# A 16-wide substitution whose blocks are joined on TensorE, as a stage of its own in the next iteration of a gated-delta-rule mixer

## Chip, cores and metric

One core of a Trainium2 chip runs the whole model, six feed-forward and mixer layers and a second model of two mixers, in one launch. The metric is the device time of one execution in microseconds. The engines are PE (TensorE; PEld is its weight load), DVE (VectorE), ACT (ScalarE), POOL (GpSimd), and SP, which issues the DMAs.

## What is computed

The change lies in one layer, the gated delta rule: 512 positions, 16 value heads of width 128 over 8 query and key heads. Cut to what matters (the kernel works in chunks of 128 positions):

```python
decay = exp(where(lower, g[..., :, None] - g[..., None, :], -inf))
kb, vb = k * beta[..., None], v * beta[..., None]
L = where(strict, einsum('bhncd,bhnsd->bhncs', kb, k) * decay, 0.0)
T = triangular_solve(eye + L, eye, lower=True, unit_diagonal=True)
u, w = T @ vb, T @ (kb * exp(g)[..., None])
...
def step(state, inp):
    v_new = u_n - w_n @ state
    o = q_n @ state + a_n @ v_new
    state = state * gl_n + k_n.T @ v_new
```

The inverse of the unit triangular matrix `eye + L`, one 128x128 block for each head and chunk, is what the edited code computes.

## The kernel before

All activations are held with the channel on the partitions, and a weight matmul is done as three in a reduced-precision format: high by high, low by high, high by low (`mm3`, L145 to L147). A weight tile comes in by SP (`raw`, three buffers), ACT rounds it to `wh` (L139) and DVE forms the rest `wl` (L140). Results land in `acc`, three banks of PSUM; DVE or ACT must read a bank before PE may fill it again.

`gdn` works in 8 groups `gi`, of one query and key head and two value heads. `stage_a` projects and convolves the group's queries and keys, normalises them (`norms`), forms their products with themselves (L1099, masked on DVE to `gt` at L1100), and from them the strictly triangular blocks `Am` (L1120, L1121, four operations on DVE) and `At` (POOL, L1122), 8 blocks of 128x128 side by side. Then it inverts. Each 128x128 block has four 32x32 blocks on its diagonal. Through DRAM (`ad`) they are laid out so that each partition holds whole 32x32 blocks (`ai`), and a substitution runs along the rows of the unknowns `ui`, which start as parts of the identity. First the two 16-wide halves are done at once, 15 steps of a product and a sum (L1142, L1144); then the upper half is tied to the lower with two large products (L1148, L1149), and 15 more steps finish it (L1151, L1153). Back through DRAM (`ud`, `uc`), a transpose on DVE gives `tcp` (L1164), and PE joins 32-wide blocks to 64 (L1180, L1185, L1188) and 64 to 128 (L1194, L1197), with ACT copying the results from the bank `mg` between (to `z32`, `tz`, `U`).

`stage_v` projects and convolves the values (transposed at L1211); `stage_b` runs the recurrence over the four chunks: `k` times the state `St` (L1238), `R` on DVE (L1240), `U` times `R` (L1243), `vnew` on ACT (L1246), the state's increment and the output (L1250 to L1254), the new `St` on DVE (L1259; L1262 a copy for the first chunk). `stage_z` is the output gate, `stage_g` normalises the output, and `stage_o` is the output projection of the group before, added into `h` on DVE (L1292), 8 times a group.

The loop emits, in iteration `gi`: values of `gi+1`, `stage_a` of `gi+2`, recurrence of `gi`, gate, norm, projection of `gi-1`. Before it stand `stage_a` of 0 and 1 and the values of 0. This order is a priority alone: a scheduler that has its own notion of how long things take places each instruction in its engine's queue when the program is built, and each engine then works strictly through its queue. Pools decide too: `Am`, `U`, `ui` have two buffers, `big` (for `ai`, the broadcast gates and the norms) three, `mg` one bank.

Of the kernel before, what the change touches and what calls it, by code (L numbers as in the profile page):

```python
# [12 lines left out]
AF = mybir.ActivationFunctionType  # L13
ALU = mybir.AluOpType
AX = mybir.AxisListType
# [951 lines left out]
def gdn(self, feed0, gate, tail):  # L967
    nc, tc, A = self.nc, self.tc, self.A
    with tc.tile_pool(name="gd", bufs=1) as gd, tc.tile_pool(name="gdd", bufs=1, space=bass.MemoryType.DRAM) as dr:
# [104 lines left out]
        def stage_a(gi):  # L1074
# [19 lines left out]
            q, k = qk  # L1094
# [33 lines left out]

            ad = dr.tile([8, 4, 32, 32], F32, name="ad", bufs=2)
# [6 lines left out]
            nc.vector.memset(ai.rearrange("p j i -> p (j i)")[:, 0:1024:33], -1.0)  # L1136
            ui = T("ui", (P, 8, 32), bufs=2)
            nc.sync.dma_start(ui, A["gdn_eye"])
            mt = T("mt", (P, 2, 4, 16), bufs=2)
# [6 lines left out]
            for v in range(2):  # L1146
                x = T("ix").rearrange("p (q i j) -> p q i j", q=4, i=8)
                nc.vector.tensor_mul(x, fdims(ui, 0, (32, 4), (0, 8), (1, 16)), fdims(ai, 16 + 8 * v, (0, 4), (1, 8), (32, 16)))  # L1148
                nc.vector.tensor_reduce(ui[:, 0:4, 16 + 8 * v:24 + 8 * v], x, axis=AX.X, op=ALU.add, negate=True)  # L1149
            for t in range(1, 16):  # L1150
                nc.vector.tensor_mul(mt[:, 0, :, :t + 1], ui[:, 0:4, 16:17 + t],  # L1151
                                     fdims(ai, 16 * 32 + 16 + t, (0, 4), (32, t + 1)))
                nc.vector.tensor_reduce(ui[:, 0:4, 16 + t:17 + t], mt[:, 0, :, :t + 1], axis=AX.X, op=ALU.add, negate=True)  # L1153
# [9 lines left out]
            tcp = T("tcp", (P, 8, 32))  # L1163
            nc.vector.transpose(tcp.rearrange("p n i -> p (n i)"), uc.rearrange("p n i -> p (n i)"))  # L1164
# [4 lines left out]
            for b in range(4):  # L1169
                sl = slice(32 * b, 32 * b + 32)  # L1170
                nc.scalar.copy(U[sl, :, sl], uc[sl])
                if b < 2:
                    nc.scalar.copy(t64[sl, :, sl], tcp[sl])
            n8 = "p (n i) -> p n i"
            z32 = T("z32", (P, 8, 32))
            pm = self.bank("mg")
            for m in range(2):
                s0, s1 = slice(64 * m, 64 * m + 32), slice(64 * m + 32, 64 * m + 64)
                for n in range(8):
                    nc.tensor.matmul(pm[s1, n * 32:(n + 1) * 32], Am[s0, n, s1], tcp[s0, n, :], start=True, stop=True)  # L1180
                nc.scalar.copy(z32[s1], pm[s1, 0:256].rearrange(n8, n=8))
# [563 lines left out]
```

## Time and profile before

| | |
|---|---|
| median of 3 runs | 2827.94 us (2823.83 to 2828.90) |
| the profiled execution | 2832.52 us |
| its span | 2830.7 us, 36488 instructions |
| mean granted clock of PE | 0.971 |
| this layer | about 1850 to 2480 us of the span |

The span is what the profile shows, from the first instruction to the last; the execution's time has 1.8 us more. An engine's busy time is the time in which one of its instructions ran. A wait is put down to the instruction whose end released it. Granted clock 1.00 is 2.4 GHz and 0.50 is 1.2 GHz.

### The profile page before, as it was taken

The numbers are of one execution on the slowest core, as the hardware profiler recorded it, in microseconds if no ns is written. First come the engines' busy times: TensorE is split into PE (matmuls) and PEld (weight loads), VectorE is DVE, ScalarE is ACT, GpSimd is POOL, SyncE is SP. The second block draws the span as 40 slices with busy tenths as digits, with TensorE's granted clock in tenths as the row PEclk, the third lists the DMA queues.
The fourth block names the chain that finished last, engine by engine and source line by source line (L and its number), as shares of the span: only waits on it lengthen the run. The fifth ranks groups of instructions, "written<-read, shape, count | busy, mean of one in ns | idle before, by whom it ended". The sixth has DMA issues, their size and how long they took to land.

```text
span 2830.7 us, 36488 instructions
## 1 busy us (share of the span) xinstructions
PE 2718.2 (96%) x13879; PEld 2218.0 (78%) x13879; DVE 1774.8 (63%) x3321; ACT 1194.0 (42%) x2192; POOL 239.4 (8%) x224
## 2 busy tenths in 40 slices
PE   8999999999999999999899999988999999999998
PEld 6888878788888888887678888876777777777776
DVE  6454577754545644358854343599778788577765
ACT  4222254532323422233463232374545444477773
POOL 0000002000000000005310000030111111120001
PEclk9999999999999999999999999999889999899999
DMA  5343332244443433322113333323223233132221
GB/s 184 116 139 108 125 93 75 90 134 120 133 127 106 137 103 97 96 87 86 50 60 94 100 95 99 92 66 113 76 86 105 88 96 89 43 99 68 78 63 62
DMA packets 106704, 274.49 MB, mean 97 GB/s; under 512 B 35465, under 2 KB 39553, under 8 KB 106529
## 3 DMA queue, kind: packets, MB, share of 16 engines
q1 hardware_dynamic: 106528, 272.15, 31.3%
q8 instruction: 110, 1.80, 0.3%
q14 instruction: 66, 0.53, 0.1%
HBM read 267.79 MB, written 4.31 MB: 96 GB/s over the span
## 4 chain that ended last, share of the span: by engine, by line
PE 35%; DVE 10%; ACT 3%; issue 1%; POOL 1%; DMA 0%; DVEq 0%; SPq 0%; POOLq 0%; ACTq 0%
PE acc L145 9%; PE acc L146 9%; PE acc L147 9%; DVE wl L140 1%; PE mg L1484 1%; POOL x L1389 1%; DVE Am L1121 1%; DVE mt L1142 0%; PE sb L1475 0%; PE mg L1185 0%; DVE Am L1120 0%; ACT wh L139 0%; PE mg L1194 0%; PE sb L1254 0%; PE sb L1243 0%
## 5 line engine op out<-in xcount | busy, mean ns | idle before, releaser
L145 PE MATMUL acc<-xh,wh 128*128 128x512 f32 (+2 forms) x2320 | 914.5, 395 | 18.9 <-ACT xh L186 8.2
L146 PE MATMUL acc<-xl,wh 128*128 128x512 f32 (+1 forms) x2320 | 906.9, 391 | 5.4 <-POOL xl L151 3.2
L147 PE MATMUL acc<-xh,wl 128*128 128x512 f32 (+1 forms) x2320 | 903.3, 390 | 2.0 <-DVE wl L140 2.0
L139 ACT CAST wh<-raw 128x1024 fp32r<-128x1024 f32 (+3 forms) x430 | 439.3, 1022 | 1076.7 <-PE acc L146 713.3
L140 DVE TENSOR_TENSOR wl<-raw,wh 128x1024 fp32r<-128x1024 f32 (+2 forms) x410 | 488.1, 1192 | 97.0 <-ACT wh L139 93.2
L145 PEld LDWEIGHTS acc<-xh,wh 128*128 128x128 f32 (+1 forms) x2320 | 438.2, 189 | 110.5 <-ACT xh L186 8.2
L146 PEld LDWEIGHTS acc<-xl,wh 128*128 128x128 f32 x2320 | 438.2, 189 | 95.0 <-POOL xl L151 4.5
L147 PEld LDWEIGHTS acc<-xh,wl 128*128 128x128 f32 x2320 | 437.6, 189 | 92.4 <-DVE wl L140 3.5
L146 PE MATMUL acc<-al,wh 128*128 128x512 f32 (+1 forms) x720 | 278.1, 386 | 0.0
L147 PE MATMUL acc<-ah,wl 128*128 128x512 f32 (+1 forms) x720 | 277.8, 386 | 0.0
L145 PE MATMUL acc<-ah,wh 128*128 128x512 f32 (+1 forms) x720 | 277.4, 386 | 0.0
L249 DVE SCALAR_TENSOR_TENSOR h<-acc,h 128x512 f32<-128x512 f32 x128 | 88.4, 690 | 215.7 <-PE acc L147 215.3
L289 DVE TENSOR_TENSOR tmp<-acc,rstd 128x512 f32<-128x512 f32 x88 | 60.9, 691 | 240.0 <-PE acc L147 240.0
L287 DVE TENSOR_TENSOR tmp<-acc,rstd 128x512 f32<-128x512 f32 x88 | 60.8, 691 | 176.2 <-PE acc L147 176.1
L146 PEld LDWEIGHTS acc<-al,wh 128*128 128x128 f32 x720 | 135.2, 188 | 28.6 <-DVE al L151 0.8
L145 PEld LDWEIGHTS acc<-ah,wh 128*128 128x128 f32 x720 | 135.2, 188 | 28.2
L147 PEld LDWEIGHTS acc<-ah,wl 128*128 128x128 f32 x720 | 135.2, 188 | 28.0
L145 PE MATMUL acc<-ogh,wh 128*128 128x512 f32 (+1 forms) x256 | 111.5, 440 | 19.4 <-DVE h L1292 19.2
L140 POOL TENSOR_TENSOR wl<-raw,wh 128x1024 fp32r<-128x1024 f32 (+1 forms) x20 | 47.8, 2393 | 872.2 <-ACT wh L139 861.2
L146 PE MATMUL acc<-ogl,wh 128*128 128x512 f32 (+1 forms) x256 | 106.4, 416 | 0.0
L147 PE MATMUL acc<-ogh,wl 128*128 128x512 f32 (+1 forms) x256 | 105.0, 410 | 0.0
L150 ACT CAST ah<-tmp 128x512 fp32r<-128x512 f32 x88 | 54.8, 623 | 63.9 <-DVE tmp L290 63.9
(448 smaller groups left out, 3589.0 us busy)
## 6 DMA issues: line engine op xcount, KB each, us to landing
raw<-in_wi_dram SPq DMA_DIRECT2D x176, 512.0 KB
raw<-in_wo_dram SPq DMA_DIRECT2D x64, 512.0 KB
raw<-in_ada_w_dram SPq DMA_DIRECT2D x48, 512.0 KB
raw<-in_a_in_dram SPq DMA_DIRECT2D x48, 512.0 KB
raw<-in_b_in_dram SPq DMA_DIRECT2D x24, 512.0 KB
raw<-in_wo_dram SPq DMA_DIRECT2D x24, 384.0 KB
raw<-in_a_out_dram SPq DMA_DIRECT2D x16, 512.0 KB
big<-rd SPq DMA_DIRECT2D x13, 512.0 KB
```

Of the source, the lines that this page charges most:

```text
L139: nc.scalar.copy(wh[:, :n], raw[:, :n])
L140: self.lo_eng.tensor_tensor(wl[:, :n], raw[:, :n], f32(wh[:, :n]), op=ALU.subtract)
L145: nc.tensor.matmul(out, ah, bh, start=start, stop=False)
L146: nc.tensor.matmul(out, ah, bl, start=False, stop=False)
L147: nc.tensor.matmul(out, al, bh, start=False, stop=stop)
L150: self.nc.scalar.copy(hi, x)
L249: nc.vector.scalar_tensor_tensor(self.h[m], ps, scale(m), self.h[m], op0=ALU.mult, op1=ALU.add)
L287: nc.vector.tensor_mul(t, pg, rstd)
L289: nc.vector.tensor_mul(u, pu, rstd)
L1121: nc.vector.tensor_mul(m, m, bcol[:, :, hs[a]:hs[a] + 1].to_broadcast([P, 4, P]))
L1389: nc.gpsimd.tensor_mul(x, x, r)
L1484: nc.tensor.matmul(po[pair[a], j * P:], vs[p][:, j, vo:vo + 64], pT[a][:, j, j * P:], start=j == 0, stop=j == 3)
```

## The change

The substitution stops after the 15 steps of the two 16-wide halves. PE joins the halves: in each of the four 32-partition strips, `Am` of the lower rows times `tcp` (L1172, 32 matmuls), an ACT copy to `z32`, `z32` times the upper half of `uc` (L1176, 32 matmuls), a subtraction on DVE (L1178) and a second transpose. The old joining then follows, with the two strips of a batch now alternating, so that its five batches of 32-wide blocks become two. All of this, from the substitution on, is a function of its own, `stage_u`. In iteration `gi` it is emitted for group `gi+1` behind the recurrence of `gi`; for group 0 it stands between the two `stage_a` ahead of the loop.

```diff
--- before.py
+++ after.py
@@ -1126,6 +1126,7 @@
                 nc.gpsimd.tensor_mul(qd[:, a], q, gbc[:, a])
 
 
             ad = dr.tile([8, 4, 32, 32], F32, name="ad", bufs=2)
             for b in range(4):
                 nc.sync.dma_start(ad[:, b].rearrange("n j i -> j n i"), Am[32 * b:32 * b + 32, :, 32 * b:32 * b + 32])
@@ -1133,9 +1134,13 @@
             adv = ad.rearrange("n b j i -> (n b) (j i)")
             for s in range(4):
                 nc.sync.dma_start(ai[32 * s:32 * s + 32].rearrange("p j i -> p (j i)"), adv)
-            nc.vector.memset(ai.rearrange("p j i -> p (j i)")[:, 0:1024:33], -1.0)
             ui = T("ui", (P, 8, 32), bufs=2)
             nc.sync.dma_start(ui, A["gdn_eye"])
+            return dict(hs=hs, k=k, knat=knat, egl=egl, ekd=ekd, At=At, qd=qd, Am=Am, ai=ai, ui=ui)
+
+        def stage_u(d):
+            Am, ai, ui = d["Am"], d["ai"], d["ui"]
+            nc.vector.memset(ai.rearrange("p j i -> p (j i)")[:, 0:1024:33], -1.0)
             mt = T("mt", (P, 2, 4, 16), bufs=2)
             for t in range(1, 16):
                 nq = (t + 3) // 4
@@ -1143,14 +1148,6 @@
                                      fdims(ai, t, (528, 2), (0, nq), (32, t + 1)))
                 nc.vector.tensor_reduce(fdims(ui, t, (144, 2), (32, nq), (1, 1)), mt[:, :, :nq, :t + 1], axis=AX.X,
                                         op=ALU.add, negate=True)
-            for v in range(2):
-                x = T("ix").rearrange("p (q i j) -> p q i j", q=4, i=8)
-                nc.vector.tensor_mul(x, fdims(ui, 0, (32, 4), (0, 8), (1, 16)), fdims(ai, 16 + 8 * v, (0, 4), (1, 8), (32, 16)))
-                nc.vector.tensor_reduce(ui[:, 0:4, 16 + 8 * v:24 + 8 * v], x, axis=AX.X, op=ALU.add, negate=True)
-            for t in range(1, 16):
-                nc.vector.tensor_mul(mt[:, 0, :, :t + 1], ui[:, 0:4, 16:17 + t],
-                                     fdims(ai, 16 * 32 + 16 + t, (0, 4), (32, t + 1)))
-                nc.vector.tensor_reduce(ui[:, 0:4, 16 + t:17 + t], mt[:, 0, :, :t + 1], axis=AX.X, op=ALU.add, negate=True)
             ud = dr.tile([8, 4, 8, 4, 32], F32, name="ud", bufs=2)
             for s in range(4):
                 nc.sync.dma_start(ud[:, :, :, s].rearrange("n b q i -> (n b) q i"), ui[32 * s:32 * s + 32])
@@ -1160,34 +1157,50 @@
             uc = T("uc", (P, 8, 32))
             for b in range(4):
                 nc.sync.dma_start(uc[32 * b:32 * b + 32], udv[b])
-            tcp = T("tcp", (P, 8, 32))
-            nc.vector.transpose(tcp.rearrange("p n i -> p (n i)"), uc.rearrange("p n i -> p (n i)"))
+            n8 = "p (n i) -> p n i"
+            z32, tcp = T("z32", (P, 8, 32)), T("tcp", (P, 8, 32))
+
+            def turned():
+                nc.vector.transpose(tcp.rearrange("p n i -> p (n i)"), uc.rearrange("p n i -> p (n i)"))
+            quart = [slice(32 * b, 32 * b + 32) for b in range(4)]
+
+            turned()
+            pm = self.bank("mg")
+            for n in range(8):
+                for q in quart:
+                    r = slice(q.start, q.start + 16)
+                    nc.tensor.matmul(pm[q, n * 32:(n + 1) * 32], Am[r, n, q], tcp[r, n, :], start=True, stop=True)
+            nc.scalar.copy(z32, pm[:, 0:256].rearrange(n8, n=8))
+            for n in range(8):
+                for q in quart:
+                    nc.tensor.matmul(pm[q, 256 + n * 16:256 + (n + 1) * 16], z32[q, n, :], uc[q, n, 16:32], start=True,
+                                     stop=True)
+            nc.vector.tensor_sub(uc[:, :, 16:32], uc[:, :, 16:32], pm[:, 256:384].rearrange(n8, n=8))
+            turned()
             lo, hi = slice(0, 64), slice(64, P)
             tz = T("tz", (P, 8, 64))
             t64, z64 = tz[lo], tz[hi]
             nc.gpsimd.memset(t64, 0.0)
-            for b in range(4):
-                sl = slice(32 * b, 32 * b + 32)
-                nc.scalar.copy(U[sl, :, sl], uc[sl])
+            for b, q in enumerate(quart):
+                nc.scalar.copy(U[q, :, q], uc[q])
                 if b < 2:
-                    nc.scalar.copy(t64[sl, :, sl], tcp[sl])
-            n8 = "p (n i) -> p n i"
-            z32 = T("z32", (P, 8, 32))
+                    nc.scalar.copy(t64[q, :, q], tcp[q])
             pm = self.bank("mg")
-            for m in range(2):
-                s0, s1 = slice(64 * m, 64 * m + 32), slice(64 * m + 32, 64 * m + 64)
-                for n in range(8):
+            both = ((quart[0], quart[1]), (quart[2], quart[3]))
+            for n in range(8):
+                for s0, s1 in both:
                     nc.tensor.matmul(pm[s1, n * 32:(n + 1) * 32], Am[s0, n, s1], tcp[s0, n, :], start=True, stop=True)
+            for s0, s1 in both:
                 nc.scalar.copy(z32[s1], pm[s1, 0:256].rearrange(n8, n=8))
-            for m in range(2):
-                s0, s1 = slice(64 * m, 64 * m + 32), slice(64 * m + 32, 64 * m + 64)
-                for n in range(8):
+            for n in range(8):
+                for s0, s1 in both:
                     nc.tensor.matmul(pm[s0, n * 32:(n + 1) * 32], z32[s1, n, :], uc[s1, n, :], start=True, stop=True)
-                if m == 0:
-                    for n in range(8):
-                        nc.tensor.matmul(pm[s1, 256 + n * 32:256 + (n + 1) * 32], uc[s1, n, :], z32[s1, n, :],
-                                         start=True, stop=True)
-                    nc.scalar.activation(t64[s1, :, s0], pm[s1, 256:512].rearrange(n8, n=8), AF.Copy, scale=-1.0)
+            s0, s1 = both[0]
+            for n in range(8):
+                nc.tensor.matmul(pm[s1, 256 + n * 32:256 + (n + 1) * 32], uc[s1, n, :], z32[s1, n, :], start=True,
+                                 stop=True)
+            nc.scalar.activation(t64[s1, :, s0], pm[s1, 256:512].rearrange(n8, n=8), AF.Copy, scale=-1.0)
+            for s0, s1 in both:
                 nc.scalar.activation(U[s0, :, s1], pm[s0, 0:256].rearrange(n8, n=8), AF.Copy, scale=-1.0)
             pm = self.bank("mg")
             for n in range(8):
@@ -1196,7 +1209,7 @@
             for n in range(8):
                 nc.tensor.matmul(pm[lo, n * 64:(n + 1) * 64], z64[:, n, :], U[hi, n, hi], start=True, stop=True)
             nc.scalar.activation(U[lo, :, hi], pm[lo].rearrange(n8, n=8), AF.Copy, scale=-1.0)
-            return dict(hs=hs, k=k, knat=knat, egl=egl, ekd=ekd, At=At, qd=qd, U=U)
+            d["U"] = U
 
         def stage_v(gi):
             hs = (2 * gi, 2 * gi + 1)
@@ -1292,7 +1305,9 @@
                     nc.vector.scalar_tensor_tensor(self.h[m], ps, gate[:, m:m + 1], self.h[m], op0=ALU.mult, op1=ALU.add)
 
         og, last = {}, []
-        st = {gi: stage_a(gi) for gi in range(2)}
+        st = {0: stage_a(0)}
+        stage_u(st[0])
+        st[1] = stage_a(1)
         vs = {0: stage_v(0)}
         for gi in range(8):
             if gi < 7:
@@ -1302,6 +1317,8 @@
             if gi == 0:
                 self.late()
             oT = stage_b(gi, st.pop(gi), vs.pop(gi))
+            if gi < 7:
+                stage_u(st[gi + 1])
             z = stage_z(gi)
             og[gi] = stage_g(gi, oT, z)
             if gi:
```

Three places in the order that the scheduler makes of it. First DVE, where the products of one group (`gt`, `Am`) meet the additions into `h` of the projection. Before, group 6's products:

```order
L1292 SCALAR_TENSOR_TENSOR h_89<-acc,mod_273,h_89 128x512
L1100 TENSOR_TENSOR gt<-sa,dmask 128x512 x2
L1120 TENSOR_TENSOR Am<-gt,tmp 128x512 x2
L1121 TENSOR_TENSOR Am<-Am,gbcol 128x512 x2
L1044 TENSOR_TENSOR nr_17816<-nr_17815 128x8
L1292 SCALAR_TENSOR_TENSOR h_90<-acc,mod_273,h_90 128x512
L1045 TENSOR_TENSOR nr_17816<-nr_17816,nr_17814 128x8
L1292 SCALAR_TENSOR_TENSOR h_91<-acc,mod_273,h_91 128x512
```

Now, the corresponding place of group 6 (L1305 is the old L1292, L1288 the old L1275):

```order
L1100 TENSOR_TENSOR gt<-sa,dmask 128x512 x2
L1120 TENSOR_TENSOR Am<-gt,tmp 128x512
L140 TENSOR_TENSOR wl<-raw,wh 128x1024
L1121 TENSOR_TENSOR Am<-Am,gbcol 128x512
L1120 TENSOR_TENSOR Am<-gt,tmp 128x512
L1121 TENSOR_TENSOR Am<-Am,gbcol 128x512
L1288 TENSOR_TENSOR oT<-oT,zg 128x512
L1016 SCALAR_TENSOR_TENSOR zg<-zg,acc 128x512
L1288 TENSOR_TENSOR oT<-oT,zg 128x512
L1305 SCALAR_TENSOR_TENSOR h_89<-acc,mod_273,h_89 128x512
L1040 TENSOR_SCALAR nr_17850<-nr_17850 128x8
```

Before, the first `h` stands ahead of the four `Am` and the other seven behind; now all eight stand behind.

Second PE, at a joining in the later groups. Before (L1180 to L1188 are batches of eight small matmuls between the large ones of a projection):

```order
L1180 MATMUL mg<-tcp,Am 32x32 x8
L146 MATMUL acc<-xl_106,wh 128x512
L147 MATMUL acc<-xh_98,wl 128x512
L145 MATMUL acc<-xh_99,wh 128x512
L146 MATMUL acc<-xl_107,wh 128x512
L147 MATMUL acc<-xh_99,wl 128x512
L1180 MATMUL mg<-tcp,Am 32x32 x8
L145 MATMUL acc<-xh_100,wh 128x512
L146 MATMUL acc<-xl_108,wh 128x512
L147 MATMUL acc<-xh_100,wl 128x512
L1185 MATMUL mg<-uc,z_15440 32x32 x8
L1188 MATMUL mg<-z_15440,uc 32x32 x8
```

Now (L1251, L1256, L1263, L1266 and L1267 are the recurrence, the old L1238, L1243, L1250, L1253 and L1254):

```order
L1256 MATMUL sb<-R,U 128x128 x2
L1172 MATMUL mg<-tcp,Am 32x32 x25
L1263 MATMUL sb<-vnew,kdec 128x128 x2
L1266 MATMUL sb<-qd,St 128x128
L1267 MATMUL sb<-At,vnew 128x128
L1266 MATMUL sb<-qd,St 128x128
L1267 MATMUL sb<-At,vnew 128x128
L1172 MATMUL mg<-tcp,Am 32x32 x2
L1061 MATMUL sa<-ident,nr_17401 8x128
L1172 MATMUL mg<-tcp,Am 32x32 x5
L147 MATMUL acc<-xh_102,wl 128x512
L145 MATMUL acc<-xh_103,wh 128x512
```

The joining of one group has moved from beside a projection into the recurrence of the group before, and its first new batch is broken up by it. Over all groups PE goes over to 32- or 64-wide matmuls 45 times before and 77 times now.

Third DVE, around the first `St` of group 0's recurrence. Before:

```order
L1022 SCALAR_TENSOR_TENSOR x_15195<-acc,pk,x_15195 128x511
L1153 TENSOR_REDUCE ui<-mt 128x4
L1022 SCALAR_TENSOR_TENSOR x_15195<-acc,pk,x_15195 128x510
L1151 TENSOR_TENSOR mt<-ui,big 128x4x11
L1022 SCALAR_TENSOR_TENSOR x_15195<-acc,pk,x_15195 128x509
L1153 TENSOR_REDUCE ui<-mt 128x4
L1262 COPY St<-sb 128x128
L1151 TENSOR_TENSOR mt<-ui,big 128x4x12
L1262 COPY St<-sb 128x128
```

Now (L1275 is the old L1262, L1253 the old L1240):

```order
L1100 TENSOR_TENSOR gt<-sa,dmask 128x512
L1120 TENSOR_TENSOR Am<-gt,tmp 128x512
L1100 TENSOR_TENSOR gt<-sa,dmask 128x512
L1121 TENSOR_TENSOR Am<-Am,gbcol 128x512
L1120 TENSOR_TENSOR Am<-gt,tmp 128x512
L1022 SCALAR_TENSOR_TENSOR cv<-acc,pk,cv 128x511
L1121 TENSOR_TENSOR Am<-Am,gbcol 128x512
L1275 COPY St<-sb 128x128 x2
L1022 SCALAR_TENSOR_TENSOR cv<-acc,pk,cv 128x510
L1253 SCALAR_TENSOR_TENSOR R<-sb,negeg,vnat 128x128 x2
```

The copies of `St` stood among steps of the substitution; now they stand directly behind the products `gt` and `Am` of group 2.

## Rows read from the trace of the kernel before

**Rows 1.** The page, part 1: busy us (share of the span) xinstructions of each engine.

```profile
PE 2718.2 (96%) x13879; PEld 2218.0 (78%) x13879; DVE 1774.8 (63%) x3321; ACT 1194.0 (42%) x2192; POOL 239.4 (8%) x224
```

**Rows 2.** Busy us by stretch: length, PE, PEld, DVE, ACT, POOL, then granted clock, DMA, GB/s.

```profile
1944.00:2450.00 506.00, 474.34 (x2958) 380.29 (x2957) 392.70 (x1049) 238.28 (x639) 64.61 (x60) 0.91 0.30 89
2160.00:2200.00 40.00, 38.43 (x215) 30.99 (x213) 39.39 (x117) 23.26 (x73) 6.05 (x6) 1.00 0.27 93
```

**Rows 3.** What PE waited for, 1944 to 2450 us: us in all, times, longest.

```profile
PE acc L145 <- DVE h L1292: 19.2, 5, 6.1
PE mg L1180 <- DVE mt L1142: 3.0, 1, 3.0
PE mg L1180 <- DVE nr L1047: 2.4, 1, 2.4
PE mg L1180 <- ACT z L1181: 1.8, 1, 1.8
...
```

**Rows 4.** Timeline of DVE ahead of one late h: start us, us, line, operation, shapes.

```profile
2195.76 0.68 DVE L1100 TENSOR_TENSOR gt<-sa,dmask 128x512 f32<-128x512 f32 x1
...
2202.62 1.62 DVE L1121 TENSOR_TENSOR Am<-Am,gbcol 128x512 f32<-128x512 f32 x1
...
2204.24 0.74 DVE L1292 SCALAR_TENSOR_TENSOR h<-acc,mod,h 128x512 f32<-128x512 f32 x1
```

**Rows 5.** Timeline of PE at the same place.

```profile
2195.16 1.06 PE L1099 MATMUL sa<-x,x 128*128 128x128 f32 x8
...
2205.03 0.80 PE L145 MATMUL acc<-ogh,wh 128*128 128x512 f32 x1 [6.01 <-DVE h L1292]
```

**Rows 6.** Busy us by stretch, as rows 2: five of seven with low clock, and all.

```profile
2019.00:2040.00 21.00, 19.01 (x136) 15.45 (x134) 14.81 (x55) 10.98 (x33) 1.17 (x2) 0.51 0.07 27
2071.00:2094.20 23.20, 23.20 (x148) 17.61 (x149) 8.49 (x25) 8.04 (x16) 0.52 (x1) 0.50 0.21 69
2135.00:2138.60 3.60, 3.21 (x8) 2.10 (x9) 3.60 (x7) 0.00 (x0) 1.92 (x2) 0.55 0.22 35
2203.80:2210.70 6.90, 5.67 (x14) 4.52 (x15) 4.89 (x13) 0.00 (x0) 0.00 (x0) 0.52 0.36 58
...
2422.00:2438.60 16.60, 16.46 (x106) 13.09 (x107) 3.39 (x5) 4.14 (x10) 0.00 (x0) 0.50 0.08 28
sum 82.40, PE 75.02 PEld 58.69 DVE 43.73 ACT 23.59 POOL 6.90; mean PE 10.72 PEld 8.38 DVE 6.25 ACT 3.37 POOL 0.99
```

**Rows 7.** Costliest groups of DVE: shapes xcount, busy us, mean ns, idle before.

```profile
L1151 DVE TENSOR_TENSOR mt<-ui,big 128x8 f32<-128x8 f32 (+14 forms) x120 | 28.2, 235 | 0.7
...
L1153 DVE TENSOR_REDUCE ui<-mt 128x4 f32<-128x8 f32 (+14 forms) x120 | 22.2, 185 | 0.7
...
L1148 DVE TENSOR_TENSOR ix<-ui,big 128x512 f32<-128x512 f32 x16 | 17.3, 1080 | 0.0
...
L1149 DVE TENSOR_REDUCE ui<-ix 128x32 f32<-128x512 f32 x16 | 11.0, 685 | 0.0
...
L1164 DVE STREAM_TRANSPOSE tcp<-uc 128x256 f32<-128x256 f32 x8 | 3.5, 440 | 1.3 <-DMA uc<-ud 1.2
```

**Rows 8.** Timeline of PE through part of one joining of blocks.

```profile
2218.91 0.40 PE L145 MATMUL acc<-xh,wh 128*128 128x512 f32 x1
2219.24 0.69 PE L1180 MATMUL mg<-tcp,Am 32*32 32x32 f32 x16
...
2220.19 0.40 PE L147 MATMUL acc<-xh,wl 128*128 128x512 f32 x1
2220.42 0.40 PE L145 MATMUL acc<-xh,wh 128*128 128x512 f32 x1
...
2221.15 0.21 PE L1188 MATMUL mg<-z,uc 32*32 32x32 f32 x1
...
2221.27 0.57 PE L1188 MATMUL mg<-z,uc 32*32 32x32 f32 x13
...
2222.11 0.40 PE L147 MATMUL acc<-xh,wl 128*128 128x512 f32 x1
```

## Prediction

> **What bounds the kernel now.** I began with the page: PE is busy 96% of the span, DVE 63% [rows 1]. PE is the engine whose time adds up, so a change is worth what it takes out of PE's idle time or half-rate time, less what it adds to PE's queue; DVE time alone is worth nothing. Second view, the busy time by stretches: the edited stage lies in 1944 to 2450 us (up to 1944, about 15 DVE steps into group 0's substitution, the instructions stand in the same order in both programs). PE is busy 475 of those 506 us, so 31 us are idle, and the mean granted clock is 0.91 [rows 2]. In 2160 to 2200 DVE is busy 39.4 of 40 us: over the shares of the whole span DVE looks free, in this stretch it is full [rows 2].
>
> Third, the waits of PE in that stretch [rows 3]: five waits for the add of `h` (L1292) make 19.2 us, the longest 6.1. The others are matmuls of the old joining of blocks that wait for DVE or ACT, and come one at a time: 3.0, 2.4 and 1.8 us are the largest.
>
> Fourth, DVE's timeline at one of the five [rows 4]: from `gt` at 2195.76 DVE works through `Am` and the substitution's last steps, and reaches `h` at 2204.24. PE had finished L1099 by 2196 and then had only the output projection, whose three accumulator banks filled; it stood still 6.01 us until that `h` freed one [rows 5]. So the wait is for DVE's queue, not for data.
>
> Last, the clock in the same stretch: in seven pieces, 82.4 us in all, it is granted at half (1.2 instead of 2.4 GHz). PE is busy 75.0 us in them, so about half of that, 37.5 us, is lost [rows 6]. Each begins behind one of those waits. The three long ones (19.0, 23.2 and 16.5 us busy) are those in which PE then worked mostly on the small matmuls of the joining.
>
> The ceiling of any gain here is 31 + 37.5 = 68 us.
>
> **Part 1: DVE sheds work.** The upper half of the 32-wide substitution goes: L1148 17.3 us, L1149 11.0, L1151 28.2, L1153 22.2, together 78.7 us or 9.8 per group [rows 7]. Added per group are a second transpose at 0.44 [rows 7] and a subtraction that the trace doesn't show; it lies between nothing and that transpose, since it handles half as many elements. DVE is lighter by 8.9 to 9.4 us per group. The steps left (L1142, L1144) move as a block from beside the recurrence to behind the `h` adds.
>
> What it is worth follows from the order. In groups 2 and later `h` now stands behind all four `Am` operations. From the end of L1099 DVE has the 8.5 us of [rows 4] less some 2 us of steps that are gone, plus a `wl`, two `oT`, a `zg` and an `h`: some 10 us. In the rows shown of that place PE's queue has 21 large matmuls at about 0.235 us (from 2220.19 to 2220.42 in [rows 8]), the last small ones and transposes, some 9 us, before the projection, and three banks (nine large matmuls, 2 us) before it needs that `h`. 11 against 10: the wait goes where it was longest. Bounds: nothing to 19.2; I take 16 back, since in the first full iteration two `Am` still stand between the first and second `h`.
>
> **Part 2: PE's queue grows.** Per group 64 matmuls are added; the trace records each small one as two instructions, so 1,024 records in all. Price, from [rows 8]: from the large matmul at 2218.91 to the second one behind the batch at 2220.19 is 1.28 us where two steps of 0.235 would do: a batch of 16 records costs 0.81. From 2220.42 to 2222.11 two batches of 16 back to back cost 1.69 - 0.47 = 1.22. So 16 more records cost 0.41 (26 ns each), and a visit to small tiles costs about 0.4 beside them. Where the two batches overlap in different column strips, six starts fall within 0.12 us, 20 ns apart. The new batches go round four strips of rows and columns. At 26 ns they cost 26.6 us, at 10 (all four overlap, twice as good as two) 10. I take 15 ns, 15 us, nearer to the overlapping pair; the old batches, now also alternating, give back about 3.
>
> Visits: in the order PE goes over to small tiles 45 times before and 77 times after, since the recurrence of the group before is woven into the joining. 32 more at 0.4 is 13 us; nothing if such a visit falls into a wait. The Trainium skill, "TensorEngine Tiling (Array Packing)", section "Tiling Modes", says that a change of tiling mode drains the engine; the 0.4 us of the rows agrees, and the rule speaks against this change. Part 2 in all: 25 us, between 10 and 39.
>
> **Part 3: the joining's chain grows.** It becomes transpose, PE, ACT copy, PE, subtraction, transpose, then the old chain, and it now runs beside the recurrence. One PE batch waits for each link, and what is queued behind it on PE waits too. Old links waited 0.5 to 3.0 us [rows 3]. I leave 2 us in each of five steady groups, 10 us. One place is worse: for group 0 the copies of `St` stand behind `gt` and the four `Am` on DVE, 8.5 us by [rows 4] with little less to do, while PE has 14 large matmuls and six others, some 5 us, before it needs `St`: 3.5 us of wait. Behind it lies group 1's joining. If the clock falls there, the row of 2019 to 2040 prices it: 9.5 us lost [rows 6]. With the first iteration's `h` wait (2.5 and its share of clock, 1.5) this makes 27 us left of the 68.
>
> **The rest.** SP: `ud` and `uc` go out as before, 4 each per group, a weight load now between them; three weights are buffered and PE waited for none [rows 3], so nothing, and at worst one wait a group like the 1.8 us row. The identity load of `ui` goes out earlier, before the last one is consumed, into the second buffer: nothing. `ai` keeps one of three `big` buffers a little longer; if that were short, `rd` would land late and DVE's `oT` with it; the steps stand right behind the `h` adds, so nothing is taken. POOL's clearing of `U` moves with the joining, off PE's path. ACT has one more copy per group in the chain of Part 3.
>
> **Sum.** 68 returned, 27 left or new, 25 added: 16 us faster. The profiled execution took 2832.5 us, so 2816.5 on its scale; it lies 4.6 above the median of the runs shown, 2827.94, and on that scale the forecast is 2812.
>
> **Rivals.**
> 1. *PE packs all four strips.* For: 20 ns already with two strips. Then Part 2 is about 12 us, and if DVE's relief leaves only 10 us of waits, 68 - 10 - 12 = 46 faster: 2782. Against: the woven order breaks the batches. The Trainium skill, "TensorE: Matmul & The Clock Gate", section "Part 3: Packing small matmuls — row/col tiling", has such tiles start about 4 ns apart; by it the added records would be 4 us and not 15. The trace has shown 20 at best.
> 2. *The clock stays low through the woven stretches* (the slower side). In the new order PE has some 20 us per group with small matmuls, the recurrence and few large ones. When the clock fell ahead of such a stretch it stayed at half for 16.6 to 23.2 us [rows 6], where behind a wait followed by dense projections it was back after 3.6 to 6.9 [rows 6]. One fall costs 8 to 11.6 us, a steady 10. Without group 0's fall, 16 + 9.5 = 25 us are in hand, so from three falls on the gain is gone. Four: 68 - 25 - 18 - 40 = 15 slower, 2843; all seven: 45 slower, 2873. For: the last of those pieces stands behind a wait of only 1.8 us [rows 3] and a few tenths more. Against: the joining near 2220 ran at full clock, with large matmuls 0.23 us apart between its batches [rows 8].
> 3. *Waits trade places.* `h` no longer waits, but each new link waits 1 to 2 us: six links, seven groups, some 40 us left instead of 27, and Part 2 at 28: no change, 2828.
> 4. *The relief doesn't reach PE*: DVE is lighter where it was idle anyway. Then only Part 2 shows, 25 slower, 2853. Against: the 6.01 us wait sits in the full stretch. This is counted with rival 2.
>
> **Chances.** Forecast or near it 0.52; rival 1 0.12; rival 3 0.14; rivals 2 and 4 together 0.22. A measurement here tells about 0.2%, 5.7 us, from no change. So faster 0.64, same 0.14, slower 0.22. The range leaves out the best of rival 1 and the upper half of rivals 2 and 4: 2784 to 2842. The cases on the faster side alone span 2784 to 2822.
>
> **What would show it.** Right: PE's waits for `h` under 5 us in all, DVE no longer full for 40 us, idle time of the stage below 20 us, batches L1172 and L1176 of 64 records taking about 1.4 us each. Wrong: pieces of half clock under the woven stretches, waits of L1172, L1176 or L1197 for DVE L1164, L1178 or ACT that add up to over 30 us, or a batch over 2 us at full clock. If PE's waits for `h` remain, Part 1 has failed.

## The result, and the profile after

The changed kernel takes **2789.68 us** (median of four runs that range from 2786.3 to 2791.48), the kernel before on the same chip 2826.49: a ratio of 0.9869, 95% interval 0.9851 to 0.9886, **37 us faster**. Beside the later experiments it was measured again: 2786.38, ratio 0.9861 (0.9843 to 0.988). The forecast was 16 us faster, 2812, with a range of 2784 to 2842. The direction was right; 16 us were forecast and 37 came.

The page of the profile, part 1, after (columns as in [rows 1]):

```profile
PE 2693.3 (97%) x14903; PEld 2201.0 (79%) x14903; DVE 1731.3 (62%) x3065; ACT 1194.9 (43%) x2200; POOL 236.1 (8%) x224
```

PE has 1,024 records more than before and is busy 25 us less: it has more to do, and does less of it at half clock. The stage by stretches (columns as in [rows 2]), from 1944 us to the second batch of the matmuls of L1056 in the stage's tail, which stands at the same point of both programs. First before:

```profile
1944.00:2467.98 523.98, 488.07 (x3038) 392.41 (x3037) 405.16 (x1089) 245.38 (x668) 67.54 (x64) 0.91 0.29 87
```

After, and below it the one long piece of half clock that is left:

```profile
1944.00:2427.69 483.69, 467.26 (x4066) 379.47 (x4065) 360.44 (x832) 246.78 (x677) 64.03 (x65) 0.98 0.33 94
2049.30:2066.00 16.70, 16.70 (x135) 12.94 (x136) 5.83 (x15) 5.52 (x13) 0.52 (x1) 0.51 0.19 52
```

The stage is 40.3 us shorter; the other 4 us between the two spans (2830.7 and 2786.4) lie behind it, where this execution met less half clock. (The profiled execution of before lay 4.6 us above the median of its runs, so the medians differ by less than the two spans.) The 40.3 split into three parts: idle time of PE (length less busy); time lost to half clock (over windows of 2 us, busy time times one less the granted clock); and the rest, the time that PE would have worked at full clock. Idle time fell from 35.9 to 16.4, loss from 42.6 to 9.9, and the rest rose from 445.4 to 457.3. So 52 us came back and **12 were added**, where the prediction had 41 and 25. The rest is good to some 3 us: four runs below with the same instructions on PE give 448.3 to 454.2.

What PE waited for in the stage, after (columns as in [rows 3]):

```profile
PE mg L1192 <- DVE nr L1040: 3.7, 1, 3.7
PE acc L145 <- DVE zg L1016: 3.2, 2, 1.7
PE sa L1061 <- DVE nr L1050: 1.9, 4, 0.6
...
```

No wait for `h` (L1305 now) is left of the 19.2 us of [rows 3]; at one of the old places PE now waits 1.7 us for `zg` (L1016), which stands directly ahead of `h` on DVE. The largest wait is a new one, of the joining, and behind it lies the one long piece of half clock shown above. This is DVE at that place (columns as in [rows 4]):

```profile
2039.90 0.68 DVE L1120 TENSOR_TENSOR Am<-gt,tmp 128x512 f32<-128x512 f32 x1
2040.50 0.44 DVE L1164 STREAM_TRANSPOSE tcp<-uc 128x256 f32<-128x256 f32 x1
2040.86 1.42 DVE L1121 TENSOR_TENSOR Am<-Am,gbcol 128x512 f32<-128x512 f32 x1
2042.20 1.77 DVE L1120 TENSOR_TENSOR Am<-gt,tmp 128x512 f32<-128x512 f32 x1
2043.89 1.78 DVE L1288 TENSOR_TENSOR oT<-oT,zg 128x512 f32<-128x512 f32 x1
2045.59 1.75 DVE L1121 TENSOR_TENSOR Am<-Am,gbcol 128x512 f32<-128x512 f32 x1
2047.26 0.68 DVE L1288 TENSOR_TENSOR oT<-oT,zg 128x512 f32<-128x512 f32 x1
2047.86 0.28 DVE L1178 TENSOR_TENSOR uc<-uc,mg 128x128 f32<-128x128 f32 x1
...
2048.72 0.43 DVE L1164 STREAM_TRANSPOSE tcp<-uc 128x256 f32<-128x256 f32 x1
```

POOL's timeline and PE's at the same place:

```profile
2040.13 3.29 POOL L1122 TENSOR_TENSOR At<-gt,tmp 128x512 f32<-128x512 f32 x2 [3.59 <-DVE gt L1100]
2043.37 3.41 POOL L1126 TENSOR_TENSOR qd<-x,big 128x512 f32<-128x512 f32 x2
```

```profile
2045.16 0.39 PE L146 MATMUL acc<-ogl,wh 128*128 128x512 f32 x1
2049.29 0.42 PE L1192 MATMUL mg<-tcp,Am 32*32 32x32 f32 x13 [3.75 <-DVE nr L1040]
```

PE waits for the second `tcp`, which ends at 2049.15 (the profile names the small `nr` step that ended last). It stands behind the subtraction L1178 on DVE, and that behind `Am` and `oT`. These take 0.68 us alone, and four of them 1.42 to 1.78 here, while POOL multiplies `At` and `qd`. The four are 4.0 us too long together, as much as the wait; a run below takes POOL out.

The two new batches are cheap. PE through one of them (columns as in [rows 8]):

```profile
2102.02 0.47 PE L147 MATMUL acc<-xh,wl 128*128 128x512 f32 x1
2102.43 0.75 PE L1172 MATMUL mg<-tcp,Am 16*32 16x32 f32 x64
2103.11 0.50 PE L145 MATMUL acc<-xh,wh 128*128 128x512 f32 x1
2103.45 0.39 PE L146 MATMUL acc<-xl,wh 128*128 128x512 f32 x1
```

Reckoned as in [rows 8], 64 records cost 1.43 - 0.47 = 0.96 us, way in and out included, hardly more than 16 records of the old joining (0.81).

### The profile page after: what moved, and what is told of

Its sections match the earlier page's. It is cut to its first block, busy times and chain, and to the rows that moved or that the text cites. A ratio compares the mean times of both kernels' runs of the same rounds, so it can differ in the third digit from the quotient of the medians.

```text
span 2786.4 us, 38307 instructions
## 1 busy us (share of the span) xinstructions
PE 2693.3 (97%) x14903; PEld 2201.0 (79%) x14903; DVE 1731.3 (62%) x3065; ACT 1194.9 (43%) x2200; POOL 236.1 (8%) x224
## 5 line engine op out<-in xcount | busy, mean ns | idle before, releaser
L145 PE MATMUL acc<-ogh,wh 128*128 128x512 f32 (+1 forms) x256 | 105.4, 413 | 5.5 <-DVE zg L1016 3.2
L146 PE MATMUL acc<-ogl,wh 128*128 128x512 f32 (+1 forms) x256 | 100.1, 392 | 0.0
```

The costliest lines, as they stand in the source:

```text
L145: nc.tensor.matmul(out, ah, bh, start=start, stop=False)
L146: nc.tensor.matmul(out, ah, bl, start=False, stop=False)
```

## The experiments

Each was timed against the kernel before on its chip (2824.01 to 2826.42). Idle, loss and rest are those of the stage as defined above, from one profile each; a visit is an unbroken run of PE on the joining's small tiles in the trace of the stage (the 85 and 63 of an expectation below count eight more behind it). Fit means a least-squares estimate of mine over 6,756 stretches between neighbouring large matmuls in six of these traces, without waits and at full clock: 0.36 us a visit, 7.2 ns a record of the new batches, 22.6 ns a record of the old 32x32 ones strip by strip, 16 ns in alternation. Another choice of stretches moves these by up to 15%.

| kernel | median us | ratio to before (95%) | idle | loss | rest | visits |
|---|---|---|---|---|---|---|
| before | 2826 | 1 | 35.9 | 42.6 | 445.4 | 45 |
| the change | 2789.7, 2786.4 | 0.9869, 0.9861 | 16.4 | 9.9 | 457.3 | 77 |
| move only | 2811.4 | 0.9959 (0.9947 to 0.997) | 36.6 | 21.4 | 448.4 | 42 |
| join only | 2780.8, 2780.1 | 0.9847, 0.984 | 20.0 | 4.7 | 453.6 | 48 |
| load back, behind | 2791.4 | 0.9885 (0.9865 to 0.9905) | 20.2 | 8.2 | 458.8 | 69 |
| load back, in front | 2830.8 | 1.0023 (1.0012 to 1.0035) | 47.1 | 25.0 | 453.2 | 49 |
| new batches twice | 2794.2 | 0.9904 (0.9886 to 0.9921) | 10.3 | 3.0 | 474.6 | 104 |
| new batches strip by strip | 2810.8 | 0.9943 (0.9928 to 0.9959) | 10.4 | 23.0 | 474.0 | 79 |
| old batches strip by strip | 2792.1 | 0.9884 (0.987 to 0.9898) | 15.6 | 7.5 | 463.5 | 77 |
| ahead of the recurrence | 2785.2 | 0.9859 (0.9843 to 0.9875) | 21.4 | 10.3 | 450.9 | 55 |
| before, POOL free | 2812.0 | 0.9957 (0.9943 to 0.9972) | 29.5 | 30.2 | 448.3 | 48 |
| join only, POOL free | **2765.1** | 0.9789 (0.9769 to 0.981) | 9.5 | 0.0 | 448.3 | 48 |
| join only, `At` on DVE | 2776.4 | 0.9818 (0.9805 to 0.9832) | 16.8 | 4.2 | 454.2 | 48 |
| the change, POOL free | 2770.1 | 0.9799 (0.9786 to 0.9812) | 7.7 | 0.0 | 454.8 | 76 |

### The two halves of the change

**Move only:** the old body of before, all of it, in `stage_u`.

```diff
-        st = {gi: stage_a(gi) for gi in range(2)}
+        st = {0: stage_a(0)}
+        stage_u(st[0])
+        st[1] = stage_a(1)
...
             oT = stage_b(gi, st.pop(gi), vs.pop(gi))
+            if gi < 7:
+                stage_u(st[gi + 1])
```

> The 32-wide substitution and the joining of before, word for word, but cut out of the stage and emitted where the change emits them, behind the recurrence of the iteration before. Theory L (DVE's load: the 9.8 us per group that left DVE are what freed PE): DVE has all of its work back, the waits only change place, at most 10 us faster than before, 2816 to 2832. Theory P (the place: behind the adds of h the block delays nobody): nearly all of the change's gain without the added matmuls, 2785 to 2798, with no wait of PE for h. Theory C (both are needed): 2798 to 2816, the waits for h gone, and waits of the joining's first matmuls for DVE over 10 us in their place.

**Join only:** the new body, called at the end of `stage_a` (its other two calls go).

```diff
-            return dict(hs=hs, k=k, knat=knat, egl=egl, ekd=ekd, At=At, qd=qd, Am=Am, ai=ai, ui=ui)
+            d = dict(hs=hs, k=k, knat=knat, egl=egl, ekd=ekd, At=At, qd=qd, Am=Am, ai=ai, ui=ui)
+            stage_u(d)
+            return d
```

> The 16-wide substitution and the joining of the change, emitted where before has it, inside the stage of queries and keys. Theory L: the gain of the change or near it, 2785 to 2800, waits of PE for h under 5 us. Theory P: DVE's steps still stand ahead of h, and PE has the added matmuls; 2815 to 2835, waits for h over 10 us. Theory C: 2798 to 2815.

By the ratios join only is 43 to 45 us faster than before, more than the whole change, and move only 12. The join alone goes 4 us beyond the time that theory L asked of it, with waits for `h` of 6.7 us where L asked for under 5. The move alone fits no theory: its time is in the range of C, but the waits for `h` are not gone. The halves do not add up; both work on the same waits. What PE waited for, move only and then join only:

```profile
PE acc L145 <- DVE h L1296: 14.2, 6, 5.7
```

```profile
PE acc L145 <- DVE h L1307: 6.7, 8, 2.4
```

In the run with the move alone the waits for `h` remain although no step of the substitution stands in front of `h` any more. DVE and PE at one of them:

```profile
2188.49 2.39 DVE L1120 TENSOR_TENSOR Am<-gt,tmp 128x512 f32<-128x512 f32 x2
2190.80 3.42 DVE L1121 TENSOR_TENSOR Am<-Am,gbcol 128x512 f32<-128x512 f32 x2
2194.14 1.40 DVE L1296 SCALAR_TENSOR_TENSOR h<-acc,mod,h 128x512 f32<-128x512 f32 x2
```

```profile
2189.95 0.40 PE L147 MATMUL acc<-ogh,wl 128*128 128x512 f32 x1
2194.94 0.80 PE L145 MATMUL acc<-ogh,wh 128*128 128x512 f32 x1 [4.59 <-DVE h L1296]
```

The four `Am` take 5.8 us where four of 0.68 would take 2.7. PE has only 12 large matmuls to do between L1099 and this wait, all of the projection itself. In the change 23 others stand ahead of the projection in the same group, and its joining is done before L1099. PE of the change there, with the first and the last of the 23:

```profile
2180.26 1.06 PE L1099 MATMUL sa<-x,x 128*128 128x128 f32 x8
...
2181.52 0.48 PE L146 MATMUL acc<-xl,wh 128*128 128x512 f32 x1
...
2186.63 0.39 PE L147 MATMUL acc<-xh,wl 128*128 128x512 f32 x1
...
2187.65 0.48 PE L145 MATMUL acc<-ogh,wh 128*128 128x512 f32 x1
```

In the five steady groups there are 0, 12, 23, 21 and 19 such matmuls in the change, and none in any of the five before or with the move alone; there the longer substitution brings the joining behind `h` (the first `tcp` of the group above comes at 2196.19). So the scheduler's order on PE changed with the edit, and the move alone did not get the order of the change.

Both kernels once more, on one chip:

> The 16-wide substitution and joining in the old place once more, to set it beside the change on one chip. If the move costs what the two separate comparisons say: 7 to 11 us faster than the change, 2777 to 2784.

> The changed kernel once more, beside the run without the move: 2786 to 2792.

2780.07 and 2786.38. Beside the join, the move costs about 6 us, a little less than expected; the intervals of the two ratios overlap, but no run of the one kernel reaches into the range of the other's.

### DVE's load, behind and in front

The same 9.8 us per group of the old upper half is computed on DVE, into a tile `vi` that nobody reads; the output stays as it is.

```diff
             mt = T("mt", (P, 2, 4, 16), bufs=2)
...
+            vi = T("vi", (P, 8, 32))
+            nc.vector.memset(vi.rearrange("p q i -> p (q i)"), 0.0)
+            for v in range(2):
...
+            for t in range(1, 16):
...
             ud = dr.tile([8, 4, 8, 4, 32], F32, name="ud", bufs=2)
```

> The changed kernel, with the upper half of the 32-wide substitution computed beside it into a tile that nobody reads: DVE gets back its 9.8 us per group, PE, ACT and the emission stay as in the change. Theory L: 2815 to 2830, the clock falls return. Theory P: within 8 us of the change, 2785 to 2798. Theory C: 2798 to 2815.

For the second run the lines stand in `stage_a`, behind `Am`, and read `Am`:

> The changed kernel with the same 9.8 us per group of idle work on DVE as the run with the load given back, but emitted where the old steps stood, behind the products Am and so in front of and among the adds of h (it computes on Am, into a tile that nobody reads). Theory Q (what counts is what stands between gt and h in DVE's queue against what PE has to do meanwhile): the waits for h are back, over 10 us, clock falls behind them, 2802 to 2828. Theory N (DVE's load does not matter in any place, PE's new order covers it): within 8 us of the change, 2783 to 2796.

Behind, the load costs some 5 us (ratio 0.9885, its interval overlaps that of the change); in front, all of the gain and 6 us more (1.0023). By the times theory P holds, and theory Q with 3 us more than it asked: DVE's load counts by its place in the queue far more than by its amount. But theory Q named the wrong wait, since `h` is late by 5.1 us only; the load delays the next group's chain of `nr` instead:

```profile
PE sb L1061 <- DVE vi L1133: 12.6, 2, 6.3
PE sb L1061 <- DVE nr L1050: 8.6, 2, 4.5
PE acc L145 <- DVE ui L1160: 5.7, 1, 5.7
PE acc L145 <- DVE h L1316: 5.1, 6, 3.2
```

The order on PE moved with the load too (49 visits, not 69, and in three of the five steady groups none of the other large matmuls ahead of the projection), so this run shows the price of the place, not one wait alone.

### The price of PE's small matmuls

```diff
+            for _ in range(2):
...
-                for n in range(8):
-                    for q in quart:
+                    for n in range(8):
+                        for q in quart:
```

(the second new batch; the first likewise)

> The changed kernel with each of the two new batches of small matmuls issued twice, back to back: 1,024 records more on PE and no new visit. By the price in the prediction, 15 ns a record, 15 us slower than the change, 2805. By the change's own profile (64 records and the way in and out in 0.96 us, of which the visit is 0.4) 9 ns a record: 9 us slower, 2799. If starts in four strips cost 4 ns: 4 us, 2794.

```diff
-            for n in range(8):
-                for q in quart:
+            for q in quart:
+                for n in range(8):
```

(both new batches)

> The changed kernel with the two new batches in another order: all eight small matmuls of one strip of rows and columns, then the next strip, instead of going round the four. Same instructions. Fitted over the stretches between large matmuls in the traces of six kernels, a new record costs 7 ns going round, one of the old joining 23 ns when one strip is done at a time and 16 in alternation, a visit 0.36 us. If going round the strips is what makes the new ones cheap, 1,024 records cost 16 ns more: 16 us slower than the change, 2802 to 2810. If it is the smaller tile (16 rows, or 16 columns), no change, 2786 to 2794.

```diff
-            for n in range(8):
-                for s0, s1 in both:
+            for s0, s1 in both:
+                for n in range(8):
```

(the old joining's first two batches in the code, L1192 and L1197; the third, L1200, has one pair of strips and stays)

> The changed kernel with the old joining's first two batches (32x32 tiles) back in the order of before, one pair of strips after the other. The prediction had the alternation give back 3 us; by the fit (23 against 16 ns, 512 records) 3.4 us. So 2792 to 2794, at the edge of what can be told; 2790 if it gives nothing, over 2800 if alternation was worth more than the fit says.

*Twice:* the time can't tell the prices apart (medians 5 to 8 us above the change, ratios 10 to 12), because the longer batches also covered the wait of L1192, and idle and loss fall by 13 us. The rest does: it rises by 17.2, and there are 27 visits more, which I had excluded; 27 x 0.36 + 1,024 x 7.2 ns = 17.1. *Strip by strip:* 21 to 24 us slower than the change, 16 expected. The rest rises by 16.7, the loss by 13.1, and idle time falls by 6.0. The 16.7 is the fit's price (22.6 against 7.2 ns, 15.8 us): going round the strips makes the new records cheap, not the small tile. PE at the first of these batches:

```profile
1963.02 0.39 PE L147 MATMUL acc<-xh,wl 128*128 128x512 f32 x1
1963.34 1.91 PE L1172 MATMUL mg<-tcp,Am 16*32 16x32 f32 x64
...
1965.85 2.48 PE L1176 MATMUL mg<-uc,z 32*32 32x16 f32 x64
```

64 records take 1.91 us in place of 0.75. *Old batches:* some 4 us slower (2792.1, ratio 0.9884), by the intervals not to be told from the change; its rest is 6.2 us higher, known to some 3, which does not contradict the 3.4.

### Where the block stands against the recurrence

```diff
+            if gi < 7:
+                stage_u(st[gi + 1])
             oT = stage_b(gi, st.pop(gi), vs.pop(gi))
-            if gi < 7:
-                stage_u(st[gi + 1])
```

> The changed kernel with the substitution and joining emitted one step earlier: still in the next iteration, but ahead of the recurrence and not behind it. In the order PE then goes over to small tiles 63 times and not 85 (rows of the order). If weaving the joining into the recurrence costs visits (0.36 us each) and hides nothing, 8 us faster than the change, 2779 to 2785. If the recurrence hid the waits of the joining's links, these waits come back: 2792 to 2805.

2785.2, 1 to 4 us faster than the change: inconclusive by time. In the profile 22 visits less take 6.4 us from the rest, and idle time rises by 5.0, so most of it goes back. But it does not go back to the joining's links, as the expectation had it: these wait 1.3 us in all, and the wait of 3.7 us is gone. What came is waits for `h` and for `nr`:

```profile
PE acc L145 <- DVE h L1305: 6.7, 4, 2.4
PE sb L1061 <- DVE nr L1050: 6.0, 3, 3.9
```

Weaving the joining into the recurrence costs visits, and the order that comes with it spares other waits, about in balance.

### DVE and POOL in each other's way

```diff
-                nc.gpsimd.tensor_mul(At[:, a * 4:(a + 1) * 4, :].rearrange("p c i -> p (c i)"), qkm, e)
+                nc.vector.tensor_mul(At[:, a * 4:(a + 1) * 4, :].rearrange("p c i -> p (c i)"), qkm, e)
...
-                nc.gpsimd.tensor_mul(qd[:, a], q, gbc[:, a])
+                nc.vector.tensor_mul(qd[:, a], q, gbc[:, a])
```

On the kernel before, on join only, on the change, and with `At` alone on join only:

> The kernel before, with the two products At and the two qd of each group computed on DVE and not on POOL. In the trace of before DVE's products Am take 1.6 to 1.75 us where POOL computes At and qd at the same time, 0.68 where it doesn't. Theory S (the two engines slow each other, and that filled DVE in front of h): DVE gets 2.7 us more per group and loses some 4 us of stretching in front of h; the waits for h fall from 19 us to under 8, 2800 to 2814. Theory L (DVE has too many instructions): DVE has more to do, nothing gained, 2820 to 2835.

> The best run so far, the 16-wide substitution and joining in the old place, with At and qd computed on DVE and not on POOL. In that run POOL's products meet oT on DVE (1.24 us each where 0.62 is the undisturbed time) and no longer Am. If what is left of the waits for h (6.7 us) comes from that, 3 to 8 us faster than that run, 2773 to 2778; if DVE's 2.7 us more per group weigh the same, 2777 to 2785.

> The changed kernel with At and qd computed on DVE and not on POOL. Theory S (POOL's products stretch Am and oT in DVE's queue, 0.68 to 1.77 us each, and so delay the subtraction that the joining waits for): the wait of 3.7 us and the clock fall behind it (8.4 us) go, 10 to 14 us faster than the change, 2773 to 2779. Theory L (DVE's queue is too long there, whoever stretches it): the four products stand in DVE's queue instead, 2.7 us, the wait stays at 2 to 4 us; 2784 to 2792.

> The 16-wide substitution and joining in the old place, with At alone on DVE and qd still on POOL. The run with both on DVE took 2765, with both on POOL 2780. If At is the one that meets Am and oT: 2763 to 2770. If qd does: 2775 to 2782. If half each: 2770 to 2775.

With both moved DVE gets four products more per group, and each of the three kernels is faster: before by 12 us, the change by 16 to 20, join only by 15, which at 2765.1 makes the fastest version of the study, 60 us faster than before. On the change and on join only this is 3 and 8 us beyond the range of the theory that fits. In the kernel before the waits for `h` fall from 19.2 to 5.0 us, as theory S had it (others came in, of `R` and of the joining, so that all idle time fell by 6.4 alone):

```profile
PE acc L145 <- DVE h L1292: 5.0, 2, 4.6
PE mg L1180 <- DVE nr L1040: 3.5, 1, 3.5
```

In join only POOL's products meet `oT` (1,244 ns in the mean, 777 before) more than the second product of `Am` (L1121: 777 ns, 1,312 before), so a part of its gain could have been this alone. But with POOL free on both sides the join is still worth 47 us by the ratios (0.9957 to 0.9789), as against 43 to 45 without. In the change the new wait and its half clock are gone: loss 0.0. Three groups of DVE, 1944 to 2450 us (columns as in [rows 7]), in the change, and below it the change with POOL free:

```profile
L1288 DVE TENSOR_TENSOR oT<-oT,zg 128x512 f32<-128x512 f32 (+1 forms) x18 | 15.8, 892 | 22.3 <-PE sb L1036 18.9 <-ACT oT L1277 3.2
L1121 DVE TENSOR_TENSOR Am<-Am,gbcol 128x512 f32<-128x512 f32 x12 | 13.0, 1080 | 0.1
L1120 DVE TENSOR_TENSOR Am<-gt,tmp 128x512 f32<-128x512 f32 x12 | 10.4, 867 | 0.8 <-ACT tmp L1118 0.8
```

```profile
L1288 DVE TENSOR_TENSOR oT<-oT,zg 128x512 f32<-128x512 f32 (+1 forms) x18 | 11.0, 627 | 3.9 <-ACT oT L1277 3.2 <-PE sb L1036 0.6
L1121 DVE TENSOR_TENSOR Am<-Am,gbcol 128x512 f32<-128x512 f32 x12 | 8.2, 687 | 0.1
L1120 DVE TENSOR_TENSOR Am<-gt,tmp 128x512 f32<-128x512 f32 x12 | 8.2, 685 | 0.1
```

DVE gives back 11.8 us in these products and takes 15.9 us of `At` and `qd`; it has more to do, and less of it at the place where PE waits. With `At` alone on DVE only 4 to 8 of the 15 us come (2776.4, in the range of the case that `qd` does the harm), and `At` itself is stretched beside `qd` (1.64 us each in the mean). The two go over together.

## Why the prediction was wrong in its size

**The step that failed** is Part 2, "25 us, between 10 and 39". Measured in the stage, 12. The count of visits was right to the last one, 45 and 77, and their price nearly (0.36 against 0.4). Too dear were the records: "I take 15 ns", where they cost 7.2 by the fit, so 1,024 cost 7 us and not 15. The choice was made "nearer to the overlapping pair" of [rows 8], two strips; four overlap better, and the strip-by-strip run, in which the order of the same matmuls is the only edit, brings the price back to that of the old batches. The Trainium skill, "TensorE: Matmul & The Clock Gate", section "Part 3: Packing small matmuls — row/col tiling", has about 4 ns between the starts of such tiles; the fit's 7.2 is nearer to it than to the 15 taken. By the fit alone Part 2 is 7.4 + 11.5 - 3.4 = 15.5; the stage shows 12, less by about as much as such a split is good to.

**The second miss** is in "68 returned, 27 left or new". Back came 52 us, not 41. Of these 11, 5 came from the tail of the stage, which I had not counted, 3.5 from what the 68 left out (up to 2450 us there are 31.7 idle and 39.8 lost, not 31 and 37.5), and 2.3 from the 27, which was nearly right in size: from 1944 to 2408 us, 14.8 us idle and 9.9 lost. But its largest item was wrong. No wait of the `St` copies came; in its place stands the wait of L1192 one iteration later, 3.7 us and a loss of 8.4, where I had 3.5 and 9.5. That the sizes agree is chance. The cause was to be seen in [rows 4]: the `Am` of 1.62 us there stood beside POOL's `qd`, and I read it as the price of an `Am`. POOL in the same trace of before:

```profile
2197.30 3.47 POOL L1122 TENSOR_TENSOR At<-gt,tmp 128x512 f32<-128x512 f32 x2 [5.63 <-ACT nrj L1038]
2200.74 2.96 POOL L1126 TENSOR_TENSOR qd<-x,big 128x512 f32<-128x512 f32 x2
```

**Part 1, point by point.** "The wait goes where it was longest": right, and all of it went, 19.2 us and not 16. That PE's time hangs on what stands in front of `h` on DVE, set against the large matmuls that PE has meanwhile (21 in the prediction, 12 to 23 in four of the five steady groups), was right. That DVE must shed the work was not shown: with the load back behind the adds the kernel keeps nearly all of its gain, and in the old place the join is enough without a move. No run holds PE's order fixed while DVE's load changes, so how much of the gain each of the two brought is not shown. And 14 of the 19.2 us of waits for `h` went in the kernel before with POOL's products alone, no substitution touched.

**Part 3** gave each link of the longer chain 2 us in five groups. Only one link waited long, the 3.7 us; the others waited 1.0 us in all, and found their operands ready behind large matmuls and the recurrence.

**The rivals.** The truth lies between the forecast and rival 1, nearer to rival 1: its time of 2782 was 4 to 8 us off, and its packing in four strips, given a chance of 0.12, is what happened. Rival 2, low clock through woven stretches, did not come: from 2070 to 2400 us the granted clock was 1.00. Rivals 3 and 4 are refuted by the waits: the links waited 4.8 us in all, and nothing waited for `h`. Of the signs named beforehand, waits for `h` under 5 us (none) and idle time under 20 (16.4) came; DVE is still nearly full in places (37.6 of its fullest 40 us, 39.6 before), and the batches took 0.75 us and not 1.4.

**What stays open:** which part of the 5 us in the stage between the change and join only is visits and which is order; what in the edit brought PE its other order ahead of the projection; and why the rest of the program behind the stage was 4 us shorter, at a higher clock, with the same instructions.

## What to carry to other kernels

When an in-order engine makes another wait, look at what stands ahead of the awaited instruction and whether each of its rows takes its undisturbed time; a row at 2.6 times its usual length is a second cause, and moving the neighbour that stretches it was worth 12 to 20 us here, beside a change worth 37. Look at what the waiting engine has to do meanwhile, too: that order can move with the edit. Batches of small matmuls that go round all strips of rows and columns cost a third of the same batches done strip by strip, by the fit; price them from the widest overlap that the new order allows, not from the old one. And test the halves of a change apart: here one half alone was at least as good as both.

## What the runs showed of the hardware that was not expected

- DVE's products of two operands in SBUF took 0.68 us alone and, in the rows above, 1.42 to 1.78 beside a POOL product; POOL's own took 1.26 to 1.76 in that trace. The adds of `h`, with one operand in PSUM, kept their 0.74 (eight of them ran beside a POOL product in the traces of before, the change and join only). The Trainium skill, "SBUF — State Buffer", section "Who interferes with whom", says that a DVE instruction with two SBUF inputs contends with a GpSimd instruction that reads SBUF; these rows agree.
- The clock fell without a wait ahead of it. In the strip-by-strip run the stage lost 23 us to half clock with only 10.4 us idle; windows of that run (columns as in [rows 2]):

```profile
2168.00:2170.00 2.00, 2.00 (x59) 1.84 (x58) 1.51 (x4) 0.89 (x2) 0.22 (x1) 1.00 0.39 139
2170.00:2172.00 2.00, 2.00 (x16) 1.44 (x15) 0.61 (x2) 0.37 (x1) 0.00 (x0) 0.89 0.00 0
2172.00:2180.00 8.00, 8.00 (x84) 7.17 (x83) 1.99 (x11) 4.16 (x16) 0.62 (x1) 0.50 0.01 2
```

PE is busy throughout. What it did ahead of the fall was a batch of small matmuls in one strip at a time, 56 records in 1.65 us. All five falls of that stage that begin after 1950 us are of this kind: none has a wait of PE in the 10 us ahead of it, and each has one of the new batches there. The change, whose batches go round the strips, has its only long fall behind the wait of 3.75 us. My reading of [rows 6], that each fall begins behind a wait, was true of that trace and no rule.
